# Four feature-major products of a mixer: weights or tokens stationary

## The chip, the cores and the metric

The kernel runs on one core of a Trainium2 chip. The metric is the time of one execution on the device in microseconds (us); a result is the median of several runs. All matmuls work on float32 values that are split in two parts (`wh` and `wl`, "high" and "low"), so that the tensor engine (PE) can take them in its faster float32 form: a product x·w is computed as xh·wh + xh·wl + xl·wh.

## The reference, cut to what matters

Two layers of a decoder for 256 tokens with 2048 features. Each layer has a mixer, a cross attention into 256 memory tokens, and a gated FFN. The change is in the mixer, whose input projection makes eleven things at once:

```python
z = h @ w_in
(g_q, g_k, g_v, g_r, g_lr, s_q, s_k, s_v, c_b, c_c, c_h) = split_cols(z, IN_SIZES)
o_a = gla_chunked(g_q, g_k, g_v, log_a)          # linear attention, needs g_q and g_k
o_a = rms_norm(o_a) * silu(g_r)
o_b = swa_with_sinks(rope(s_q), rope(s_k), s_v)  # softmax attention in a window
o_c = c_b * causal_dwconv(c_c * c_h, sc_conv)    # short gated convolution
return concat([o_a, o_b, o_c]) @ w_out
```

`h` is the input after an RMS norm. The kernel multiplies by the norm's row factor only after the product. g_k and g_q have 256 columns each, g_r, c_b, c_c and c_h 512 each: 2560 columns, which are the four feature-major products (keys with queries, c_c with c_h, c_b, g_r).

## The kernel before

All weights stream from memory once. `stream` loads a tile `raw` of 128 x 1024 (four buffers) on SP's DMA queue, and ACT casts it to `wh` (L160) while DVE computes `wl` (L161), three buffers each; both carry a priority.

Two forms of product use the stream. `xstat` holds 128 tokens of x as the stationary operand and lets 512 weight columns move: three matmuls for each half of the tokens and each 128 rows of K, so 6 x 16 = 96 for 512 output columns. Its result has tokens on the partitions. `wstat` holds 128 x 128 weights and lets the tokens move, high and low part of 256 tokens at once: 512 columns with `wh`, 256 with `wl`. A group of 256 output columns is 32 such pairs, and the result has features on the partitions, with the low part's share in a second half that `fold` adds (ACT copy L257, DVE add L258). `by_row` (L262) multiplies by the row factor.

Where features are wanted on the partitions after `xstat`, `turn` (L216) does it: DVE transposes blocks of 32 x 32 from PSUM (L226, two instructions for 512 columns), one DMA writes the result to DRAM (L228), and four read it back in another order (L230). `turned_by_row` (L238) multiplies by the row factor and restores the order within a row. The memory keys (`kp`), the cross queries (`qp`) and the FFN's up-projection (`up`) work so.

Small work is written as generators that `start` puts into a list of tasks. `pump` is called after each three matmuls of `xstat` and each four of `wstat`; it lets every waiting task count down by one and advances the first one that is free to its next `yield`, whose number says how many calls it then waits. `until` calls `pump` until given tasks are done. Behind all this a scheduler orders each engine's instructions at compile time; every engine then runs its own in that order.

The mixer's order is: `tokp` (columns that stay with tokens on the partitions), two `zkq` groups, two `zq` groups (softmax queries), four `zc`, two `zb`, two `zr`, then the memory keys and the output projection. `gla` (linear attention), `swa_keys`, `swa_queries`, `swa` (softmax attention) and `memory` (memory operands, loaded after the softmax tasks) run as tasks meanwhile. The uses of the feature-major groups (row factor, `conv`, gates) stand in the program right behind their product.

Of the kernel before, what the change touches and what calls it, by code (L numbers as in the profile page):

```python
# [9 lines left out]
F32 = mybir.dt.float32  # L10
# [3 lines left out]
AF = mybir.ActivationFunctionType  # L14
ALU = mybir.AluOpType
AX = mybir.AxisListType

P = 128
D = 2048
T = 256  # L20
KT = D // P
# [7 lines left out]
C_MIX, C_X, C_MEM, C_FFN = 0, 16, 32, 48  # L29
# [17 lines left out]
WPRIO = 100  # L47
# [3 lines left out]
W = dict(lr=3, gate=1, kq=7, lv=4, att=1, norm=7, kr=3, qr=4, p=8, pT=4,  # L51
         ms0=4, ms=8, xq=4, xp=8, xv=1, row=9, up=22, nx=24, up1=3, ss1=20, ss=9)
# [20 lines left out]
class Trunk:  # L73
# [24 lines left out]

    def pump(self):

        free = None
        for task in self.tasks:
            if not all(t.done for t in task.after):
                continue
            if task.wait > 0:
                task.wait -= 1
            elif free is None:
                free = task
        if free is not None:
            try:  # L110
                free.wait = (next(free.gen) or 1) - 1
            except StopIteration:
                free.done = True
                self.tasks.remove(free)

    def until(self, *tasks):
        while not all(task.done for task in tasks):
# [28 lines left out]
    def stream(self, wd, gc, kt, keep=0):  # L146
# [3 lines left out]
        for k in range(kt):  # L150
# [10 lines left out]
                    nc.vector.tensor_tensor(wl[:, :n], raw[:, :n], wh.bitcast(F32)[:, :n], ALU.subtract)  # L161
            o = (k % kp) * gc
            yield k, wh[:, o:o + gc], wl[:, o:o + gc]

    def wstat(self, xs, wd, kt=KT, name="mm", n=2):

        nc = self.nc
        ps = self.pmm.tile([P, 2, 512], F32, tag="mm", name=name)
        for k, wh, wl in self.stream(wd, n * P, kt):
            x = xs(k // 2) if callable(xs) else xs[k // 2]  # L170
            xhl = x[:, k % 2, :, :].rearrange("p a t -> p (a t)")
            xh = x[:, k % 2, 0, :]
            for m in range(n):
                ms = slice(m * P, (m + 1) * P)
                if k < kt - 1:
                    nc.tensor.matmul(ps[:, m, :], lhsT=wh[:, ms], rhs=xhl, start=(k == 0), stop=False)
                    nc.tensor.matmul(ps[:, m, 0:T], lhsT=wl[:, ms], rhs=xh, start=False, stop=False)
                else:
                    nc.tensor.matmul(ps[:, m, 0:T], lhsT=wl[:, ms], rhs=xh, start=False, stop=False)
                    nc.tensor.matmul(ps[:, m, :], lhsT=wh[:, ms], rhs=xhl, start=False, stop=True)  # L180
            self.pump()
        return ps

    def xstat(self, xs, wd, gc=512, name="mm", kt=KT):

# [60 lines left out]
            return out[j]  # L246
        return operand


    def fold(self, ps, name="z", z=None):  # L250

        nc = self.nc
        b = self.scratch(name + "_b", (P, 2, T))
        if z is None:
            z = self.ev.tile([P, 2, T], F32, tag="evz", name=name)
        with self.tc.high_priority(offset=WPRIO):
            nc.scalar.copy(b, ps[:, :, T:2 * T])  # L257
            nc.vector.tensor_tensor(z, ps[:, :, 0:T], b, ALU.add)  # L258
        return z

    def by_row(self, z, rbc):
        self.nc.vector.tensor_tensor(z, z, rbc.unsqueeze(1).broadcast_to([P, 2, T]), ALU.mult)  # L262

    def split(self, hi, lo, src):
        self.nc.scalar.copy(hi, src)
# [156 lines left out]
    def gla(self, l, tok, kq, ready, o_sb):  # L422

        nc = self.nc
# [20 lines left out]
        b = self.big("b", [P, 512])  # L445
# [1 line left out]
            s = slice(c * 64, c * 64 + 64)  # L447
            nc.vector.tensor_tensor_scan(b[:, s], mn[:, s], ab[:, s], 0.0, ALU.add, ALU.subtract)
        while not ready:
            yield 1  # L450
        yield W["kq"]
        kz, qz = kq[:, 0, :], kq[:, 1, :]
        sc = 1.0 / 16.0
# [66 lines left out]
        for hp in range(2):  # L520
            for tb in range(2):
                for par in range(2):
                    rows = slice(par * 64, par * 64 + 64)
                    nc.tensor.matmul(pb[par][0:64, hp, tb, :], lhsT=kd[rows, hp, 2 * tb, :],
                                     rhs=qd[rows, hp, 2 * tb + 1, :], start=True, stop=True)
# [9 lines left out]
        for hp in range(2):  # L535
            for par in range(2):
                rows = slice(par * 64, par * 64 + 64)
                nc.tensor.matmul(pf[par][:, hp, :], lhsT=kd[rows, hp, 0:2, :].rearrange("p c s -> p (c s)"),
                                 rhs=qd[rows, hp, 2:4, :].rearrange("p c s -> p (c s)"), start=True, stop=True)
# [17 lines left out]
        for tb in range(2):  # L557
            for hd in range(4):
                hp, par = hd // 2, hd % 2
                if tb:  # L560
                    nc.tensor.matmul(pos[1][:, hd, :], lhsT=far[:, par, hp, :], rhs=vals[0][:, hd, :],
                                     start=True, stop=False)
                nc.tensor.matmul(pos[tb][:, hd, :], lhsT=am[:, par, hp, tb, :], rhs=vals[tb][:, hd, :],
                                 start=(tb == 0), stop=True)
# [128 lines left out]
    def mixer(self, l, xs, ss, after):  # L693
        nc, a = self.nc, self.a
        tok = [self.big(f"tok{tb}", [P, 2 * TOKC]) for tb in range(2)]
        rc, rbc, rt = self.row_factor(ss, "rx", W["ss1"] if l else 1, after)
        pst = self.xstat_both(xs, a["w_tok"][l], name="tokp")
        self.layer_rest(l)
        fm = lambda g, name: self.fold(self.wstat(xs, a["w_fm"][l, g], name=name), name)
        if l:  # L700
            self.until(rt)
        with self.tc.high_priority(offset=WPRIO):
            for c in range(2):
                for tb in range(2):
                    dst = tok[tb][:, c * TOKC:(c + 1) * TOKC]
                    if l:
                        nc.scalar.activation(dst, pst[c][tb], AF.Copy, scale=rc[:, tb:tb + 1])
                    else:
                        (nc.vector.tensor_copy if tb else nc.scalar.copy)(dst, pst[c][tb])
        z0 = fm(0, "zkq")  # L710
        if l == 0:
            self.until(rt)
            for tb in range(2):
                nc.scalar.activation(tok[tb], tok[tb], AF.Copy, scale=rc[:, tb:tb + 1])
        qsc = self.par.tile([P, 4], F32, tag="qs", name="qs")
        nc.vector.tensor_scalar(qsc[:, 0:2], rc, 0.125, None, ALU.mult)
        nc.vector.tensor_scalar(qsc[:, 2:4], rc, -0.125, None, ALU.mult)
        kq, o_sb = self.big("kq", [P, 2, 512]), self.big("o", [P, 4, T])
        ready = []
        tg = self.start(self.gla(l, tok, kq, ready, o_sb))  # L720
        if l == 0:
            self.rope_tables()
        for g in range(2):
            z = fm(g, "zkq") if g else z0
            nc.vector.tensor_tensor(kq[:, g, :].rearrange("p (h t) -> p h t", h=2), z,
                                    rbc.unsqueeze(1).broadcast_to([P, 2, T]), ALU.mult)
        nc.scalar.mul(kq[:, 1, :], kq[:, 1, :], 0.125)
        ready.append(True)
        kp, vp = self.operand("kp"), self.actp.tile([P, 2, 2, 2, P], F32R, tag="act", name="vp")
        tk = self.start(self.swa_keys(tok, kp, vp))  # L730
        ob, ts = [], []
        q = [self.big("q", (P, 2, 512)) for _ in range(2)]
        self.claim(*q)
        for g in range(2):
            qs, qTs = self.swa_rope(q[g], self.xstat(xs, a["w_q"][l, g], name="zq"), qsc), []
            og = []
            ob.append(og)
            tq = self.start(self.swa_queries(qs, qTs))
            ts += [self.start(self.swa(g, n, qTs, kp, vp, og), tk, tq) for n in range(2)]
        if l == 0:  # L740
            self.tm = self.start(self.memory_factor())
        ys, oc = self.big("cy", [P, 4, T]), [self.operand(f"oc{g}") for g in range(2)]
        self.claim(ys, *oc)
        for j in range(4):
            z = fm(4 + j, "zc")
            self.by_row(z, rbc)
            self.conv(j, z[:, 0, :], z[:, 1, :], ys[:, j, :])
        ms = []
        self.start(self.memory(l, ms), *ts)
        for g in range(2):  # L750
            z = fm(8 + g, "zb")
            self.by_row(z, rbc)
            nc.vector.tensor_tensor(z, z, ys[:, 2 * g:2 * g + 2, :], ALU.mult)
            self.split(oc[g][:, :, 0, :], oc[g][:, :, 1, :], z)
        zr, oa = self.big("zr", [P, 2, 2, T]), [self.operand(f"oa{g}") for g in range(2)]
        for g in range(2):
            z = self.fold(self.wstat(xs, a["w_fm"][l, 2 + g], name="zr"), "zr", zr[:, g])
            self.by_row(z, rbc)
        ts.append(self.start(self.gla_out(o_sb, zr, oa), tg, *ts))
        return oc + oa, ob, ts, ms  # L760

    def gla_out(self, o_sb, zr, oa):

# [132 lines left out]
    def memory(self, l, ms):  # L896
        nc = self.nc
        for j in range(0, 8, 2):
            raw = self.raw.tile([P, 2, 2, T], F32, tag="raw", name="mem")
            nc.sync.dma_start(raw, self.a["mem"][j // 2])  # L900
            x = [self.operand(f"ms{j + i}") for i in range(2)]
            self.claim(*x)
            ms += x
            yield W["ms0"]
            for i in range(2):
                self.prep(raw[:, i], self.p[:, C_MEM:C_MEM + 16], j + i, x[i])
                yield W["ms"]

    def cross_keys(self, l, ms):
# [164 lines left out]
def _groups(w, gc):  # L1074

    d, k, n = w.shape
    w = w.reshape(d, k // P, P, n // gc, gc).transpose(0, 3, 2, 1, 4)
    return np.ascontiguousarray(w).reshape(d, n // gc, P, (k // P) * gc)
# [12 lines left out]
def _layout(inp):  # L1091
# [4 lines left out]
    fm = [gk, gq, gr]  # L1096
    for j in range(4):
        fm += [cc[j * P:(j + 1) * P], ch[j * P:(j + 1) * P]]
    w_in = inp["w_in"]
    d = {}  # L1100
    d["w_tok"] = _groups(w_in[:, :, np.concatenate([lr, sk, sv, gv])], 2 * TOKC)[:, 0]
    d["w_fm"] = _groups(w_in[:, :, np.concatenate(fm + [cb])], 2 * P)
    d["w_q"] = _groups(w_in[:, :, heads], 512)
    ro = np.arange(2048)
    rows = np.concatenate([ro[1536:], ro[:512],
# [60 lines left out]
```

## Time and profile before

| | |
|---|---|
| median of 3 runs | 2840.64 us (2839.71 to 2843.66) |
| profiled execution, its time | 2840.81 us |
| its span, first to last instruction | 2839.0 us |
| PE busy, DVE busy, ACT busy | 99%, 67%, 51% of the span |
| TensorE clock granted, mean | 0.998 |
| matmuls | 13554 |
| moved | 616.97 MB, mean 217 GB/s |

A matmul's drawn length overlaps that of the next, so a PE that is busy all the time may still lose time between starts. The distance between starts is what tells the rate. Waits in the profile are put down to the last semaphore that came.

### The profile page before, as it was taken

To read this page: it belongs to the slowest core of one execution; us is meant where nothing else is said; L and a number is where in the kernel's file an instruction comes from. 1 tells how busy PE (TensorE), PEld (TensorE's weight loads), DVE (VectorE), ACT (ScalarE), POOL (GpSimd) and SP (SyncE) were. 2 spreads that over 40 slices of the span, in tenths; PEclk is the share of its full clock that TensorE was granted. 3 is DMA by queue.
4 is the path that set the end of the run, shared out by engine and by line. 5 is a ranking of instruction groups with operands and counts; after the bars stand their busy time and mean duration, and the time that the engine had idled before them with its cause. 6 is when DMAs were issued, how large, how long until landed. Compare 5 with 4: busy or idle time off the path is not lost.

```text
span 2839.0 us, 37045 instructions
## 1 busy us (share of the span) xinstructions
PE 2822.7 (99%) x13554; PEld 2362.7 (83%) x13554; DVE 1888.9 (67%) x2879; ACT 1445.1 (51%) x2060; POOL 15.8 (1%) x44
## 2 busy tenths in 40 slices
PE   9999999999999999999999999999999999999998
PEld 9888888888888888888888888888888888888886
DVE  6886665556777777755568866655567777777445
ACT  6665454445555555544455644544455555555333
POOL 0000000000000000000000000000000000000001
PEclk9999999999999999999999999999999999999999
DMA  7457777657777777766664577775677777777665
GB/s 265 153 167 224 240 242 228 182 166 246 246 230 248 244 243 235 245 208 208 202 191 149 165 230 236 240 221 172 191 233 247 243 241 238 244 239 247 195 194 155
DMA packets 207030, 616.97 MB, mean 217 GB/s; under 512 B 23520, under 2 KB 65024, under 8 KB 206848
## 3 DMA queue, kind: packets, MB, share of 16 engines
q1 hardware_dynamic: 206848, 614.61, 69.0%
q8 instruction: 106, 1.74, 0.3%
q14 instruction: 76, 0.62, 0.1%
HBM read 570.48 MB, written 44.04 MB: 216 GB/s over the span
## 4 chain that ended last, share of the span: by engine, by line
PE 97%; DVE 2%; ACT 1%; DMA 0%; issue 0%; SPq 0%; ACTq 0%; DVEq 0%
PE up L194 11%; PE up L193 11%; PE up L195 11%; PE fin L832 8%; PE res L195 7%; PE res L194 7%; PE res L193 7%; PE tokp L211 2%; PE qp L194 2%; PE vp L193 2%; PE vp L195 2%; PE vp L194 2%; PE qp L193 2%; PE qp L195 2%; PE kp L195 2%; PE kp L194 2%
## 5 line engine op out<-in xcount | busy, mean ns | idle before, releaser
L161 DVE TENSOR_TENSOR wl<-raw,wh 128x1024 fp32r<-128x1024 f32 (+1 forms) x992 | 1200.1, 1212 | 781.8 <-ACT wh L160 779.9
L160 ACT CAST wh<-raw 128x1024 fp32r<-128x1024 f32 (+1 forms) x992 | 1034.8, 1045 | 1137.0 <-PE up L195 324.5
L194 PE MATMUL up<-wl,xs 128*128 128x512 f32 x1408 | 548.2, 389 | 0.0
L193 PE MATMUL up<-wh,xs 128*128 128x512 f32 x1408 | 547.8, 389 | 0.0
L195 PE MATMUL up<-wh,xs 128*128 128x512 f32 x1408 | 547.7, 389 | 0.0
L193 PEld LDWEIGHTS up<-wh,xs 128*128 128x128 f32 x1408 | 264.3, 188 | 55.2
L194 PEld LDWEIGHTS up<-wl,xs 128*128 128x128 f32 x1408 | 264.3, 188 | 55.1 <-DVE wl L161 0.5
L195 PEld LDWEIGHTS up<-wh,xs 128*128 128x128 f32 x1408 | 264.3, 188 | 54.6
L832 PE MATMUL fin<-wh,a 128*128 128x512 f32 x704 | 189.9, 389 | 0.0
L832 PEld LDWEIGHTS fin<-wh,a 128*128 128x128 f32 x704 | 132.2, 188 | 27.5
L193 PE MATMUL res<-wh,a 128*128 128x512 f32 x352 | 136.9, 389 | 0.0
L195 PE MATMUL res<-wh,a 128*128 128x512 f32 x352 | 136.9, 389 | 0.0
L194 PE MATMUL res<-wl,a 128*128 128x512 f32 x352 | 136.9, 389 | 0.0
L832 PE MATMUL fin<-wl,a 128*128 128x512 f32 x352 | 110.0, 389 | 0.0
L1028 ACT ACTIVATE u<-z_t,par 128x256 f32<-128x256 f32 x176 | 91.5, 591 | 31.5 <-DVE z_t L238 30.8
L193 PE MATMUL vp<-wh,ms 128*128 128x512 f32 x256 | 100.3, 392 | 0.0
L193 PE MATMUL qp<-wh,xs 128*128 128x512 f32 x256 | 100.2, 391 | 0.0
L194 PE MATMUL qp<-wl,xs 128*128 128x512 f32 x256 | 100.0, 390 | 0.0
L194 PE MATMUL vp<-wl,ms 128*128 128x512 f32 x256 | 99.9, 390 | 0.0
L195 PE MATMUL vp<-wh,ms 128*128 128x512 f32 x256 | 99.9, 390 | 0.0
L195 PE MATMUL qp<-wh,xs 128*128 128x512 f32 x256 | 99.8, 390 | 0.0
L193 PE MATMUL res<-wh,xo 128*128 128x512 f32 x256 | 99.6, 389 | 0.0
(318 smaller groups left out, 4309.3 us busy)
## 6 DMA issues: line engine op xcount, KB each, us to landing
raw<-in_wu SPq DMA_DIRECT2D x352, 512.0 KB, 4.6
raw<-in_wd SPq DMA_DIRECT2D x176, 512.0 KB, 4.2
raw<-in_w_fm SPq DMA_DIRECT2D x80, 512.0 KB, 4.6
raw<-in_wk SPq DMA_DIRECT2D x64, 512.0 KB, 4.0
raw<-in_wo SPq DMA_DIRECT2D x64, 512.0 KB, 4.3
raw<-in_wq SPq DMA_DIRECT2D x64, 512.0 KB, 4.3
raw<-in_wv SPq DMA_DIRECT2D x64, 512.0 KB, 3.6
raw<-in_wxo SPq DMA_DIRECT2D x64, 512.0 KB, 4.0
```

Of the source, the lines that this page charges most:

```text
L160: nc.scalar.copy(wh[:, :n], raw[:, :n])
L161: nc.vector.tensor_tensor(wl[:, :n], raw[:, :n], wh.bitcast(F32)[:, :n], ALU.subtract)
L193: nc.tensor.matmul(ps[:, tb, :gc], lhsT=xh, rhs=wh, start=(k == 0), stop=False)
L194: nc.tensor.matmul(ps[:, tb, :gc], lhsT=xh, rhs=wl, start=False, stop=False)
L195: nc.tensor.matmul(ps[:, tb, :gc], lhsT=xl, rhs=wh, start=False, stop=(k == kt - 1))
L211: nc.tensor.matmul(out[c][tb], lhsT=lhs, rhs=w[:, c * TOKC:(c + 1) * TOKC], start=(k == 0 and i == 0), stop=(k == KT - 1 and i == 2))
L832: nc.tensor.matmul(ps[c][tb], lhsT=lhs, rhs=w[v][:, c % 2 * 512:c % 2 * 512 + 512], start=(k == 0 and n == 0), stop=(k == FT - 1 and n == 2))
L1028: nc.scalar.activation(u[:, s, :], z[:, s, :], AF.Identity, bias=self.p[:, C_FB + m:C_FB + m + 1], scale=tap[2])
```

## The change

The 2560 feature-major columns are laid out in five groups of 512 instead of ten of 256, and all of them go through `xstat`, `turn` and `turned_by_row`; `wstat`, `fold` and `by_row` are gone. The uses become tasks (`gated`), which start after the row factor's task and wait `W["up"]` = 22 calls of `pump` before they touch the turned data. The order of groups becomes 0 (keys and queries), two `zq` groups, 2 and 3 (convolution), 4 (its gate), 1 (silu gate). `pump` advances up to two free tasks in a call instead of one. `gla` asks for its keys and queries every third call instead of at each. The scaling of `tok` in layer 0 becomes a task behind the row factor, and the list of memory operands is filled as each is prepared, with `mem` pumping until the one that is asked for is there. The diff, cut to its core:

```diff
     def pump(self):
-        free = None
+        free = []
         for task in self.tasks:
             if not all(t.done for t in task.after):
                 continue
             if task.wait > 0:
                 task.wait -= 1
-            elif free is None:
-                free = task
-        if free is not None:
+            elif len(free) < 2:
+                free.append(task)
+        for task in free:
...
-    def wstat(self, xs, wd, kt=KT, name="mm", n=2):
...
-    def fold(self, ps, name="z", z=None):
...
-    def by_row(self, z, rbc):
...
         while not ready:
-            yield 1
+            yield 3
...
-        z0 = fm(0, "zkq")
-        if l == 0:
-            self.until(rt)
-            for tb in range(2):
-                nc.scalar.activation(tok[tb], tok[tb], AF.Copy, scale=rc[:, tb:tb + 1])
...
+        def scales():
+            if l == 0:
+                for tb in range(2):
+                    nc.scalar.activation(tok[tb], tok[tb], AF.Copy, scale=rc[:, tb:tb + 1])
+            nc.vector.tensor_scalar(qsc[:, 0:2], rc, 0.125, None, ALU.mult)
+            nc.vector.tensor_scalar(qsc[:, 2:4], rc, -0.125, None, ALU.mult)
+            yield 1
+
+        rt = self.start(scales(), rt, first=True)
+        group = lambda g, name, then: self.start(self.gated(
+            self.turn(self.xstat(xs, a["w_fm"][l, g], name=name), name), rbc, then), rt)
...
-        for g in range(2):
-            z = fm(g, "zkq") if g else z0
-            nc.vector.tensor_tensor(kq[:, g, :].rearrange("p (h t) -> p h t", h=2), z,
-                                    rbc.unsqueeze(1).broadcast_to([P, 2, T]), ALU.mult)
-        nc.scalar.mul(kq[:, 1, :], kq[:, 1, :], 0.125)
-        ready.append(True)
+
+        def keys_queries(z):
+            yield from z(kq.rearrange("p g (h t) -> p (g h) t", h=2))
+            nc.scalar.mul(kq[:, 1, :], kq[:, 1, :], 0.125)
+            ready.append(True)
+
+        group(0, "zkq", keys_queries)
+        self.until(rt)
...
-        for j in range(4):
-            z = fm(4 + j, "zc")
-            self.by_row(z, rbc)
-            self.conv(j, z[:, 0, :], z[:, 1, :], ys[:, j, :])
+        def channels(g, z):
+            z = yield from z()
+            for i in range(2):
+                self.conv(2 * g + i, z[:, 2 * i, :], z[:, 2 * i + 1, :], ys[:, 2 * g + i, :])
+                yield 1
+
+        def gates(z):
+            z = yield from z()
+            for g in range(2):
+                w = self.scratch("zy", (P, 2, T))
+                nc.vector.tensor_tensor(w, z[:, 2 * g:2 * g + 2], ys[:, 2 * g:2 * g + 2, :], ALU.mult)
+                self.split(oc[g][:, :, 0, :], oc[g][:, :, 1, :], w)
+                yield 1
+
+        tc = [group(2 + g, "zc", lambda z, g=g: channels(g, z)) for g in range(2)]
         ms = []
         self.start(self.memory(l, ms), *ts)
-        for g in range(2):
-            z = fm(8 + g, "zb")
...
+        ts.append(group(4, "zb", gates))
...
+        tr = group(1, "zr", lambda z: z(zr.rearrange("p g h t -> p (g h) t")))
+        ts.append(self.start(self.gla_out(o_sb, zr, oa), tg, tr, *ts))
+
+        def mem(j):
+            while len(ms) <= j:
+                self.pump()
+            return ms[j]
+
+        return oc + oa, ob, ts, mem
+
+    def gated(self, turned, rbc, then):
+        zf, zt = turned
+        def fetch(z=zt):
+            yield W["up"]
+            self.turned_by_row(z, zf, rbc)
+            return z
+        yield from then(fetch)
+        yield 1
```

## Rows read from the trace of the kernel before

**Rows 1.** The page: engines' busy time, and TensorE's granted clock in 40 slices.

```profile
PE 2822.7 (99%) x13554; PEld 2362.7 (83%) x13554; DVE 1888.9 (67%) x2879; ACT 1445.1 (51%) x2060; POOL 15.8 (1%) x44
...
PEclk9999999999999999999999999999999999999999
```

**Rows 2.** Timeline of PE: start, length, line, form; four stretches' first and last.

```profile
41.95 0.39 PE L176 MATMUL zkq<-xs,wh 128*128 128x512 f32 x1
...
50.26 0.39 PE L176 MATMUL zkq<-xs,wh 128*128 128x512 f32 x1
...
739.62 0.39 PE L193 MATMUL up<-wh,xs 128*128 128x512 f32 x1
...
761.38 0.39 PE L193 MATMUL up<-wh,xs 128*128 128x512 f32 x1
...
1636.48 0.39 PE L176 MATMUL zr<-xs,wh 128*128 128x512 f32 x1
...
1644.95 0.40 PE L176 MATMUL zr<-xs,wh 128*128 128x512 f32 x1
```

**Rows 3.** Waits of PE in the whole span: us in total, times, longest.

```profile
PE zq L194 <- DVE wl L161: 1.9, 2, 1.3
...
PE zr L177 <- DVE wl L161: 0.8, 1, 0.8
PE zr L176 <- ACT wh L160: 0.4, 1, 0.4
```

**Rows 4.** Windows: us, busy PE, PEld, DVE, ACT, POOL, PEclk, DMA, GB/s.

```profile
66.00:126.00 60.00, 59.35 (x498) 48.00 (x497) 51.20 (x141) 37.81 (x82) 0.21 (x3) 1.00 0.48 148
126.00:185.00 59.00, 59.00 (x347) 51.35 (x346) 48.95 (x139) 38.71 (x89) 0.48 (x6) 1.00 0.53 170
185.00:215.00 30.00, 29.86 (x174) 25.63 (x173) 25.44 (x45) 19.14 (x36) 0.18 (x2) 1.00 0.54 169
...
700.00:1179.00 479.00, 479.00 (x2116) 396.37 (x2115) 359.40 (x535) 258.86 (x355) 0.00 (x0) 1.00 0.75 241
```

**Rows 5.** Groups by line and form, 42 to 239 us: busy us, mean ns, idle.

```profile
L161 DVE TENSOR_TENSOR wl<-raw,wh 128x1024 fp32r<-128x1024 f32 x57 | 69.3, 1220 | 19.1 <-ACT wh L160 18.9
...
L258 DVE TENSOR_TENSOR zc<-zc,zc_b 128x512 f32<-128x512 f32 x4 | 2.7, 683 | 0.1
...
L257 ACT COPY zc_b<-zc 128x512 f32<-128x512 f32 x4 | 2.3, 584 | 0.0
```

**Rows 6.** Lines 226 and 238: ns min/median/max, and DVE's idle time before.

```profile
L226 DVE STREAM_TRANSPOSE z_t<-up x88: 668/690/717, 721.5 to 2588.5; 128x512 f32<-128x512 f32 x88
...
L238 DVE TENSOR_TENSOR z_t<-z,rxb x88: 681/686/695, 732.0 to 2615.2; 128x512 f32<-128x512 f32 x88
...
  DMA z<-z_d: 38.0, 39
```

**Rows 7.** DMA issues: count, KB each, median us to landing.

```profile
z<-z_d SPq DMA_DIRECT2D x240, 128.0 KB, 3.1
```

**Rows 8.** Waits of SP's DMA queue: us in total, times, longest.

```profile
SPq L230 <- DMA z_d<-z_t: 173.0, 60, 3.8
SPq L228 <- DVE z_t L226: 79.4, 60, 2.2
```

**Rows 9.** The chain that ended last, in order of time: start, us, what.

```profile
75.22 0.50 PE a L492 x22
...
85.08 1.15 DVE wl L161
...
1482.93 1.14 DVE wl L161
```

**Rows 10.** Tile ob, the softmax attention's output: durations, first and last start.

```profile
L266 DVE TENSOR_TENSOR ob<-ov,ob x16: 411/416/425, 149.7 to 1619.4; 128x256 fp32r<-128x256 f32 x16
```

**Rows 11.** Tile ms, the memory operands: durations, first and last start.

```profile
L279 DVE SCALAR_TENSOR_TENSOR ms<-mem,par,ms x32: 472/478/485, 206.8 to 1641.0; 128x256 fp32r<-128x256 f32 x32
```

**Rows 12.** Timeline of ACT, 207 to 222 us; in brackets idle time and releaser.

```profile
217.14 1.71 ACT L278 ACTIVATE ms<-mem,par 128x256 fp32r<-128x256 f32 x4 [4.30 <-DMA mem<-in_mem]
```

More of the change, by code (lines that the diff above doesn't have):

```diff
@@ L106, in pump @@
                 task.wait -= 1
-            elif free is None:
-                free = task
-        if free is not None:
+            elif len(free) < 2:
+                free.append(task)
+        for task in free:
             try:
-                free.wait = (next(free.gen) or 1) - 1
+                task.wait = (next(task.gen) or 1) - 1
             except StopIteration:
-                free.done = True
-                self.tasks.remove(free)
+                task.done = True
+                self.tasks.remove(task)
     def until(self, *tasks):
@@ L163, in stream @@
             yield k, wh[:, o:o + gc], wl[:, o:o + gc]
-    def wstat(self, xs, wd, kt=KT, name="mm", n=2):
[L167 to L182, printed above, removed]
     def xstat(self, xs, wd, gc=512, name="mm", kt=KT):
@@ L247, in when @@
         return operand
-    def fold(self, ps, name="z", z=None):
[L252 to L259, printed above, removed]
-    def by_row(self, z, rbc):
-        self.nc.vector.tensor_tensor(z, z, rbc.unsqueeze(1).broadcast_to([P, 2, T]), ALU.mult)
     def split(self, hi, lo, src):
@@ L698, in mixer @@
         self.layer_rest(l)
-        fm = lambda g, name: self.fold(self.wstat(xs, a["w_fm"][l, g], name=name), name)
         if l:
@@ L709, in mixer @@
                         (nc.vector.tensor_copy if tb else nc.scalar.copy)(dst, pst[c][tb])
-        z0 = fm(0, "zkq")
-        if l == 0:
-            self.until(rt)
-            for tb in range(2):
-                nc.scalar.activation(tok[tb], tok[tb], AF.Copy, scale=rc[:, tb:tb + 1])
-        qsc = self.par.tile([P, 4], F32, tag="qs", name="qs")
-        nc.vector.tensor_scalar(qsc[:, 0:2], rc, 0.125, None, ALU.mult)
-        nc.vector.tensor_scalar(qsc[:, 2:4], rc, -0.125, None, ALU.mult)
+        qsc = self.par.tile([P, 4], F32, tag="qs", name="qs")
+        def scales():
[8 more added lines that the diff above has]
+            self.turn(self.xstat(xs, a["w_fm"][l, g], name=name), name), rbc, then), rt)
         kq, o_sb = self.big("kq", [P, 2, 512]), self.big("o", [P, 4, T])
         ready = []
-        tg = self.start(self.gla(l, tok, kq, ready, o_sb))
+        tg = self.start(self.gla(l, tok, kq, ready, o_sb), rt)
         if l == 0:
             self.rope_tables()
-        for g in range(2):
-            z = fm(g, "zkq") if g else z0
-            nc.vector.tensor_tensor(kq[:, g, :].rearrange("p (h t) -> p h t", h=2), z,
-                                    rbc.unsqueeze(1).broadcast_to([P, 2, T]), ALU.mult)
-        nc.scalar.mul(kq[:, 1, :], kq[:, 1, :], 0.125)
-        ready.append(True)
+        def keys_queries(z):
[4 more added lines that the diff above has]
+        self.until(rt)
         kp, vp = self.operand("kp"), self.actp.tile([P, 2, 2, 2, P], F32R, tag="act", name="vp")
-        tk = self.start(self.swa_keys(tok, kp, vp))
+        tk = self.start(self.swa_keys(tok, kp, vp), rt)
         ob, ts = [], []
@@ L743, in mixer @@
         self.claim(ys, *oc)
-        for j in range(4):
-            z = fm(4 + j, "zc")
-            self.by_row(z, rbc)
-            self.conv(j, z[:, 0, :], z[:, 1, :], ys[:, j, :])
+        def channels(g, z):
[11 more added lines that the diff above has]
+        tc = [group(2 + g, "zc", lambda z, g=g: channels(g, z)) for g in range(2)]
         ms = []
         self.start(self.memory(l, ms), *ts)
-        for g in range(2):
-            z = fm(8 + g, "zb")
-            self.by_row(z, rbc)
-            nc.vector.tensor_tensor(z, z, ys[:, 2 * g:2 * g + 2, :], ALU.mult)
-            self.split(oc[g][:, :, 0, :], oc[g][:, :, 1, :], z)
-        zr, oa = self.big("zr", [P, 2, 2, T]), [self.operand(f"oa{g}") for g in range(2)]
[L756 to L760, printed above, removed]
+        ts.append(group(4, "zb", gates))
+        zr, oa = self.big("zr", [P, 2, 2, T]), [self.operand(f"oa{g}") for g in range(2)]
+        tr = group(1, "zr", lambda z: z(zr.rearrange("p g h t -> p (g h) t")))
[13 more added lines that the diff above has]
+        yield 1
     def gla_out(self, o_sb, zr, oa):
@@ L902, in memory @@
             self.claim(*x)
-            ms += x
             yield W["ms0"]
             for i in range(2):
-                self.prep(raw[:, i], self.p[:, C_MEM:C_MEM + 16], j + i, x[i])
+                ms.append(self.prep(raw[:, i], self.p[:, C_MEM:C_MEM + 16], j + i, x[i]))
                 yield W["ms"]
@@ L1101, in _layout @@
     d["w_tok"] = _groups(w_in[:, :, np.concatenate([lr, sk, sv, gv])], 2 * TOKC)[:, 0]
-    d["w_fm"] = _groups(w_in[:, :, np.concatenate(fm + [cb])], 2 * P)
+    d["w_fm"] = _groups(w_in[:, :, np.concatenate(fm + [cb])], 512)
     d["w_q"] = _groups(w_in[:, :, heads], 512)
```

## The prediction, made before the change was run

> **What bounds the kernel now.** I read the page first: PE is busy 2822.7 of 2839.0 us [rows 1], and the granted clock is full from start to end. That row alone says only that the tensor engine sets the time; a matmul is drawn with 389 ns while the next one starts after 227 ns, so a short stall doesn't show in it. So I went to the starts of the matmuls. In the FFN's up-projection, which already has the form that the change gives to the mixer (activations stationary, 512 weight columns moving), 96 matmuls take from 739.62 to 761.38 us: 21.76 us, 226.7 ns each [rows 2]. 512 columns at the full clock of 2.4 GHz are 213.3 ns, so each matmul carries 13.4 ns beside its columns. In the mixer's feature-major groups (weights stationary) a pair of a 512-column and a 256-column matmul takes 346.3 ns in the first group (24 pairs, 41.95 to 50.26) and 352.9 ns in the last (24 pairs, 1636.48 to 1644.95) [rows 2]. Its 768 columns are 320.0 ns: two fixed parts of about 13 ns, and in some groups 6.6 ns more.
>
> The waits of PE come next. Apart from the warm-up they are 1.9 us at zq, 0.8 and 0.4 at zr: four in all, each for a split weight (the ACT cast `wh` or the DVE difference `wl`) [rows 3]. Since 389 - 227 = 162 ns of each is hidden by the drawn length, what they cost is 3.1 + 4 x 0.16 = 3.7 us. All lie in the mixer. There DVE, not the transfers, is near its limit: 51.2 of 60 us, 49.0 of 59, 25.4 of 30, against 359.4 of 479 in the FFN, where the DMA share is higher (0.75 against about 0.5) and PE waits for nothing [rows 4].
>
> So the stake is small: the matmuls' fixed parts in ten 512-column groups, and a few stalls.
>
> **The matmuls.** Removed per layer: ten 256-column groups of 32 pairs, in two layers 640 pairs (1280 matmuls). Added: five groups of 96, in two layers 960 matmuls. Both stream the same 491,520 columns, so only fixed parts differ. Bounds for a pair: 346.3 and 352.9 ns; I take the middle, 349.6, since groups of both kinds are about equally common. 640 x 0.3496 = 223.7 us go and 960 x 0.2267 = 217.6 us come: **6.1 us less** (4.0 with the lower pair, 8.2 with the upper) [rows 2].
>
> The trace prices the fixed part at 13.4 ns [rows 2]. The Trainium skill (TensorE: Matmul & The Clock Gate, section Back-to-back issue gap) speaks against the change here: it gives a warm gap of N/2.4 ns plus 2.5 ns, by which 320 instructions fewer would be worth 320 x 2.5 ns = 0.8 us, an estimate from that page. The trace doesn't agree with it: 226.7 ns at 512 columns.
>
> **The evacuation.** Removed per 256 columns: an ACT copy (584 ns), a DVE add (683) and a DVE multiply of the same shape [rows 5]. Added per 512 columns: two DVE block transposes (690 each) and two multiplies by the row factor (686) [rows 6]. DVE: 4 x 0.683 = 2.73 us before, 2 x 0.690 + 2 x 0.686 = 2.75 after: nothing. ACT: 2 x 0.584 = 1.2 us less per group, 12 us over the kernel, off the path. The keys' and queries' multiply, the convolution and the gate multiply keep their element counts. PSUM keeps two buffers of two banks; one is to be emptied in 21.8 us instead of 11.1. The two transposes need 1.4 us, so this costs nothing.
>
> **The turn through DRAM.** Ten turns more, each one write of 512 KB and four reads of 128 KB on SP's queue, behind which the weight loads stand. The reads land 3.1 us after issue [rows 7], and SP stands 173.0 us in 60 turns (2.9 each) until the write is there, 79.4 us (1.3 each) for the transposes [rows 8]. So a turn holds the weights' queue for about 4.2 us, plus the issues. Cover: four raw tiles of 2.72 us of PE each (12 matmuls), and up to three split ones. The FFN does just this every 21.8 us with no PE wait [rows 3, 4]; the mixer gets the same cadence. I take nothing; if that cover is gone, a turn costs up to its 4.2 us, 42 us in all, which the FFN's rows speak against.
>
> **The later start of the linear attention.** Its keys and queries now come whole after 41.6 + 21.8 = 63.4 us (the first pair starts 0.35 us before the 41.95 of [rows 2]), and their use waits 22 steps of three matmuls (0.68 us): 15 us, more than write and reads need, then 7 steps more: about 83 us instead of 75.2 [rows 9]. Its output is wanted by the output projection alone, which comes after the four streams of the memory keys (4 x 21.8 us), so 8 us are covered: nothing. The convolution, gate and silu groups have their results turned within the next stream; the last (zr) turns under the memory keys, 87 us long: nothing. The tok scaling of layer 0 moves behind the row factor; its bound is the one wait at zq that it adjoins, 1.3 us.
>
> **Two tasks at each step.** The step hands out work; it adds none. Attention chains that shared one slot now advance together, so the softmax ends earlier (in layer 1 its last output came at 1619.4 us [rows 10]), and the memory operands, which wait for it and were prepared until 1641.0 us [rows 11], 4 us before the last zr matmuls of [rows 2] end, come earlier: a wait less likely, never seen here. The price is order: DVE and ACT run theirs in a fixed order. At 217 us ACT stood 4.3 us for a load of `mem` [rows 12], the casts of `wh` behind it came late, and PE paid the zr waits. Such stalls are bounded below by none (3.7 us gained) and above by the rivals. As DVE's load stays the same and ACT's falls slightly, I take about as much stall as before: 0.
>
> Sum: -6.1 us. The profiled execution took 2840.81 us, 0.17 above the median: 2840.81 - 6.1 = 2834.7, as a median 2834.5 us (-0.22%). Less than 0.2%, 5.7 us, is about what can't be told from no change.
>
> **Rivals.**
> *Stalls vanish.* Earlier use and less ACT work keep `wh` and `wl` ahead: -6.1 - 3.7 = -9.8, 2831. For it: the FFN runs this form clean [rows 3]. Against: the mixer's DVE share, 83 to 85% against 75% [rows 4].
> *The wait for turned data takes the gain.* The multiply by the row factor waits for the reads on DVE: 39 times, 38.0 us, in the kernel before [rows 6]; `wl` queues behind it. If half of the ten turns lose what the late `mem` did (0.8 + 0.4 + 0.3 = 1.5 us), it is 7.5 us: 2842, no change.
> *DVE is overrun: slower.* Splitting weights takes DVE 69.3 us of the 197 from 42 to 239 [rows 5], 21 us in each 60, so tasks are 30 of the 51.2 us in 66 to 126 and 28 of the 49.0 in 126 to 185 [rows 4]. Two tasks at a time pull the second share forward. A third of it (9 us) just fills the first stretch; with half, 5 us spill over, in both layers 10; with two thirds, 10 and 20: 2840.6 - 6.1 + 20 = 2854. It decides from half on. For it: at 85 us and 1482 us, where PE waited for zq, the chain that ended last runs through DVE's `wl` [rows 9]. Against: the splits have priority, so the work that spills is the tasks' own.
> *The new form runs slower in the mixer.* If its matmuls there take 233 ns, as the pairs of the last group are slower than those of the first by 6.6 [rows 2], 960 of them need 223.7 us and nothing is won: 2840.6, no change. Against: none of the FFN's do. The Trainium skill's 2.5 ns of the page above would end at the same place (2839.8 us, by its 0.8 us).
>
> **Chances.** Stalls as before, within 2 us: 0.41, of which 0.24 lie beyond -5.7 us. Stalls gone: 0.24. Turned data late: 0.20. DVE overrun: 0.12. Slower matmuls: 0.03. Faster 0.24 + 0.24 = 0.48; no change 0.17 + 0.20 + 0.03 = 0.40; slower 0.12. The range: down to 2828.5 (no stalls with the upper pair: 2840.6 - 8.2 - 3.7), up to 2846, which holds the late data and the overrun up to half; the rest of the overrun is left out. The likeliest case alone: 2830.5 to 2838.5.
>
> **What would show it.** 20 transposes and 20 more multiplies by the row factor, 70 writes and 280 reads of turned data; no fold; 96 matmuls in 21.8 us in each quiet group; the first product of the linear attention near 83 us; the softmax's last output of layer 1 well before 1619 us. Wrong would be: pairs' fixed part not the cause (groups slower than 21.8 us without a wait), PE waits for `wl` or `wh` above 10 us, or PE waiting for `ms` at the start of the memory keys.

## The result and the profile after

The changed kernel takes 2855.24 us (median of 6 runs, 2854.09 to 2856.39), the kernel before, beside it, 2839.69 (2839.40 to 2843.66): a ratio of 1.0054, 95% interval 1.0044 to 1.0064. It is slower by half a per cent. The prediction (2834.5, range 2828.5 to 2846) had the wrong sign, and the measured time lies outside the range.

The profiled spans are 2839.0 us before and 2853.0 after. The first part of the page, after:

```profile
PE 2829.8 (99%) x13234; PEld 2353.6 (82%) x13234; DVE 1890.7 (66%) x2879; ACT 1435.6 (50%) x2040; POOL 15.8 (1%) x44
```

320 matmuls are gone as planned, DVE's work is the same and ACT's is 10 us less [rows 1]. The span is 14 us longer with less to do, so the loss is in waits and in the rate. The waits of PE, after, apart from the warm-up (us in total, times, longest):

```profile
PE zr L175 <- DVE wl L161: 4.0, 2, 2.6
PE zr L174 <- ACT wh L160: 2.4, 2, 1.6
PE zc L175 <- DVE wl L161: 2.3, 1, 2.3
PE zq L175 <- DVE wl L161: 0.9, 1, 0.9
PE zb L175 <- DVE wl L161: 0.6, 1, 0.6
PE zc L174 <- ACT wh L160: 0.5, 1, 0.5
```

Against [rows 3]: zr had 1.2 us and has 6.4; zc and zb had none. Around the waits at zc (142.9 us) and at zr (231.6 us; 1643 and 1646 us) the granted clock falls. Windows after (us, PE, PEld, DVE, ACT and POOL busy, clock, DMA share, GB/s):

```profile
118.00:139.00 21.00, 20.46 (x150) 15.73 (x148) 14.64 (x46) 14.30 (x45) 0.35 (x3) 1.00 0.47 151
139.00:146.00 7.00, 4.44 (x12) 2.95 (x11) 7.00 (x17) 4.54 (x8) 0.00 (x0) 0.55 0.54 153
232.00:235.00 3.00, 3.00 (x9) 2.32 (x8) 3.00 (x5) 2.41 (x4) 0.00 (x0) 0.50 0.97 272
1645.00:1651.00 6.00, 4.82 (x11) 3.80 (x12) 6.00 (x9) 3.12 (x5) 0.00 (x0) 0.50 0.68 216
```

At 0.50 (1.2 GHz) a matmul of 512 columns starts 0.43 us after the last, where 0.23 us is usual at the full clock. The timeline of PE after shows it behind the wait at zc, and, in a quiet stretch of the keys' group, two rows that are 12 matmuls apart: 2.72 us, 226.7 ns each:

```profile
59.13 0.39 PE L176 MATMUL zkq<-wh,xs 128*128 128x512 f32 x1
...
61.85 0.39 PE L176 MATMUL zkq<-wh,xs 128*128 128x512 f32 x1
...
142.86 0.80 PE L175 MATMUL zc<-wl,xs 128*128 128x512 f32 x1 [2.26 <-DVE wl L161]
143.45 0.63 PE L176 MATMUL zc<-wh,xs 128*128 128x512 f32 x1
143.88 0.63 PE L174 MATMUL zc<-wh,xs 128*128 128x512 f32 x1
```

I set the distance from each matmul's start to the next against (columns + 32)/2.4 GHz, which gives 226.7 ns at 512 columns, and added up the excess. The span's +14.0 us divide so:

| | before | after | difference, us |
|---|---|---|---|
| fixed parts: 320 matmuls fewer at 13.3 ns | | | -4.3 |
| excess where PE waited | 4.6 | 13.0 | +8.3 |
| excess in the three stretches at half clock (17 us long) | 0 | 6.1 | +6.1 |
| excess between small matmuls of tasks | 8.9 | 13.9 | +5.0 |
| excess within the ten feature-major groups | 4.5 | 4.7 | +0.2 |
| all else | | | -1.3 |

The fourth line holds no wait that the profile shows. It grows where two tasks' matmuls alternate. In layer 1, after, one transpose of the softmax (`pT`, 128 columns) and then two to four products of the linear attention (`a`, 32 columns) follow each other at 0.20 to 0.26 us, where (columns + 32)/2.4 GHz gives 0.07 us for a transpose and 0.03 for a product; 22 such products in one run took 0.50 us before [rows 9]. That the switch itself costs is an argument: a wait shorter than the drawn length doesn't show here.

```profile
1554.38 0.27 PE L645 MATMUL pT<-con,pr 128*128 128x128 f32 x1
1554.58 0.30 PE L459 MATMUL a<-e 64*64 64x32 f32 x4
1554.82 0.33 PE L645 MATMUL pT<-con,pr 128*128 128x128 f32 x1
1555.08 0.30 PE L459 MATMUL a<-e 64*64 64x32 f32 x2
1555.31 0.33 PE L645 MATMUL pT<-con,pr 128*128 128x128 f32 x1
```

**What comes later.** The tile `ob`, after (durations, first to last start):

```profile
L233 DVE TENSOR_TENSOR ob<-ov,ob x16: 414/418/425, 159.8 to 1649.9; 128x256 fp32r<-128x256 f32 x16
```

And the splits of the memory operands `ms`, in the view of the tile `mem`:

```profile
L246 DVE SCALAR_TENSOR_TENSOR ms<-mem,par,ms x32: 473/478/485, 224.2 to 1654.7; 128x256 fp32r<-128x256 f32 x32
```

The softmax's last output came at 1619.4 [rows 10] and comes at 1649.9; the memory operands' last split came at 1641.0 [rows 11] and comes at 1654.7. In layer 0 the linear attention's products `a` end at 165.3 us instead of 108.9, the last `ob` is at 236.5 instead of 213.8, the first `ms` at 223.5 instead of 205.2, while the memory keys start only 11 us later (246.7 for 235.7).

**The wait at zc (142 us).** ACT's groups after, 129.5 to 137.5 us: sixteen exponentials, each with a read of its sum, in a row:

```profile
L631 ACT ACTIVATE pr<-pr,swc 128x256 f32<-128x256 f32 x8 | 4.0, 501 | 0.0
L631 ACT ACTIVATE pr<-pr,swc 128x128 f32<-128x128 f32 x8 | 3.1, 388 | 0.0
L631 ACT ACTIVATION_READ_ACCUMULATOR pr<-pr,swc 128x1 f32 x16 | 3.0, 190 | 0.0
```

The cast before them began at 129.13, the next at 137.56, though its raw tile had landed at 132.96. Three split buffers are 3 x 2.72 = 8.2 us of PE; the distance is 8.4 us here and up to 10.7 elsewhere, before never above 8.2.

The longer part of the wait is DVE's. PE took the cast at 138.65 us, ran four transposes and then stood 2.26 us for `wl`, until 142.86. DVE ran eight scalings of the softmax (`pr`) and four operations of the linear attention (`e`) first:

```profile
138.13 2.19 DVE L638 TENSOR_SCALAR pr<-pr,swc 128x256 f32<-128x256 f32 x8
140.24 0.42 DVE L440 TENSOR_TENSOR e<-b 128x256 f32<-128x256 f32 x1
...
141.58 1.22 DVE L161 TENSOR_TENSOR wl<-raw,wh 128x1024 fp32r<-128x1024 f32 x1
```

So it is at all five waits for `wl`, 7.8 us of the 10.7: the cast was done 0.7 to 3.0 us before DVE began on `wl`, and DVE did tasks' work or stood for turned data in between.

**The waits at zr.** The timeline of ACT, after, around 220 us:

```profile
217.85 1.05 ACT L160 CAST wh<-raw 128x1024 fp32r<-128x1024 f32 x1 [1.12 <-PE zb L176]
223.02 0.58 ACT L232 CAST pT<-pT 128x512 fp32r<-128x512 f32 x1 [4.12 <-PE pT L645]
223.50 2.91 ACT L245 ACTIVATE ms<-mem,par 128x256 fp32r<-128x256 f32 x7
...
226.57 2.11 ACT L245 ACTIVATE ms<-mem,par 128x256 fp32r<-128x256 f32 x5
228.58 2.12 ACT L160 CAST wh<-raw 128x1024 fp32r<-128x1024 f32 x2
```

And SP's, of the same stretch:

```profile
216.77 0.33 SPq L897 DMA_DIRECT2D mem<-in_mem  x1
219.52 0.33 SPq L209 DMA_DIRECT2D zb_d<-zb_t  x1
220.62 0.48 SPq L158 DMA_DIRECT2D raw<-in_w_fm  x1
222.69 1.75 SPq L211 DMA_DIRECT2D zb<-zb_d  x4
225.94 5.96 SPq L158 DMA_DIRECT2D raw<-in_w_fm  x4
```

Three loads of `mem` (issued at 170.9, 196.6 and 216.8 us) sit in three of the four raw buffers until their twelve preparations run, in a row, from 223.50 to 228.7. One buffer is left for weights: one load goes out at 220.62, the next at 225.94, after the turn of zb. No weight is cast between 217.85 and 228.58. Before, at most two were lent, and the preparations came as 8, 4 and 4.

In layer 1, at 1646.18 us, `wl` came late for turned data as well. ACT had ended the cast at 1643.06; DVE then stood for the reads of zb and multiplied them by the row factor before it split:

```profile
1637.96 4.83 DVE L246 SCALAR_TENSOR_TENSOR ms<-mem,par,ms 128x256 fp32r<-128x256 f32 x12
1643.70 1.29 DVE L219 TENSOR_TENSOR zb_t<-zb,rxb 128x512 f32<-128x512 f32 x2 [0.90 <-DMA zb<-zb_d]
1644.91 1.22 DVE L161 TENSOR_TENSOR wl<-raw,wh 128x1024 fp32r<-128x1024 f32 x1
```

### The profile page after: what moved, and what is told of

Its sections match the earlier page's. It is cut to its first block, busy times and chain, and to the rows that moved or that the text cites. A ratio compares the mean times of both kernels' runs of the same rounds, so it can differ in the third digit from the quotient of the medians.

```text
span 2853.0 us, 36449 instructions
## 1 busy us (share of the span) xinstructions
PE 2829.8 (99%) x13234; PEld 2353.6 (82%) x13234; DVE 1890.7 (66%) x2879; ACT 1435.6 (50%) x2040; POOL 15.8 (1%) x44
## 4 chain that ended last, share of the span: by engine, by line
PE 96%; DVE 1%; ACT 1%; DMA 1%; issue 0%; SPq 0%; ACTq 0%; DVEq 0%
PE up L175 11%; PE up L176 11%; PE up L174 11%; PE fin L829 8%; PE res L176 7%; PE res L174 7%; PE res L175 7%; PE tokp L192 2%; PE qp L175 2%; PE vp L175 2%; PE vp L174 2%; PE qp L176 2%; PE vp L176 2%; PE qp L174 2%; PE kp L174 2%; PE kp L175 2%
## 5 line engine op out<-in xcount | busy, mean ns | idle before, releaser
L174 PE MATMUL vp<-wh,ms 128*128 128x512 f32 x256 | 100.2, 392 | 0.0
L174 PE MATMUL qp<-wh,xs 128*128 128x512 f32 x256 | 100.2, 391 | 0.0
```

Source lines behind the costliest of these rows:

```text
L174: nc.tensor.matmul(ps[:, tb, :gc], lhsT=xh, rhs=wh, start=(k == 0), stop=False)
```

## The experiments

The theories. **Order:** two tasks a step and the later use of the keys let small work come in rows that outlast the split buffers (theory P of the expectations). **Lent buffers:** `mem` and `memt` hold raw buffers that the weights need (theory R). **Queue:** ten more turns stand between weight loads on SP (theory T). **Form:** the product is itself slower here. Each kernel has 3 rounds, and its ratio is to the kernel before beside it (2839.4 to 2840.5 us).

**One part alone.** `one_task`: the new form, one task a step; its linear attention still asks for its keys every third call. `two_before`: the old form, two tasks, and asking every third call.

```diff
# one_task, on the kernel after
-elif len(free) < 2:
+elif len(free) < 1:
# two_before, on the kernel before
-elif free is None:
-    free = task
+elif len(free) < 2:
+    free.append(task)
...
-    yield 1
+    yield 3
```

> The changed kernel with one task advanced at a step instead of two; products and turns stay. Its PE waits are 10.7 us and three stretches at half clock cost about 8.5 us more. Theory R (weight tiles starve because memory loads sit in the stream's raw buffers while ACT is late): fewer late preparations, PE waits of 3 to 7 us, 2838 to 2848. Rival P (two tasks at a step bunch the work on ACT and DVE): the stalls go back to those of the kernel before, 2833 to 2840. Rival T (the turns hold the weights' queue): stalls stay, above 2850.

> The kernel before, weights stationary, with two tasks advanced at a step and the linear attention asking every third call. Theory P: the stalls come with the two tasks, 2848 to 2860. Theory T: the stalls need the turns, so no change, 2836 to 2843. Theory R alone: some more waits because the memory loads come earlier, 2840 to 2850.

Measured: 2846.27 (1.0021 [1.0012, 1.0030]) and 2848.59 (1.0031 [1.0019, 1.0043]). Each part alone costs, 6.6 and 8.9 us, and their sum is the 15.5 us of the change. That is no proof that they are independent: asking every third call is in both kernels, the excess between small matmuls rises by 0.4 us in `two_before` and 2.0 in `one_task`, but by 5.0 with both, and with five raw buffers (below) the two don't add up. In `two_before` PE waits 4.2 us at zc in two waits; the longer (2.9) comes behind two casts at 1526.33 and 1538.28 with sixteen exponentials between them. So the two tasks cost without the new form, and the late `mem` is not needed for it.

**The raw buffers.** `raw5` has five of them, `mem_own` four and one more for `mem` and `memt` alone; `before_raw5` (with two `evz` buffers, to make room) and `before_raw3` do it to the kernel before, `one_raw5` to `one_task`.

```diff
-self.raw = pool("raw", 4)
+self.raw = pool("raw", 5)
-... self.raw.tile([P, 2, 2, T], F32, tag="raw", name="mem")
+... self.raw.tile([P, 2, 2, T], F32, tag="mem", name="mem", bufs=1)
```

> The changed kernel with five raw buffers instead of four, the memory loads still among them. Theory R: one more weight tile ahead while memory tiles are held, the waits fall by about half, 2840 to 2850. Rival P: 2850 to 2857, since ACT is late whatever is loaded. Rival T: a turn of 4.2 us on the queue is then covered, 2836 to 2845.

> The changed kernel with one buffer of its own for the memory loads (mem and memt), so that the four raw buffers hold weights alone. Theory R: the waits of PE for wh and wl at zc and zr fall from 9.8 us to under 4, the clock stays at full, 2835 to 2843. Rivals P and T: ACT and DVE are as bunched, the queue as held, 2850 to 2857.

> The kernel before with five raw buffers (and two instead of three for the sums of fold, to make room). If a fifth raw tile helps any form of this kernel, its own 3.1 us of waits for split weights go and it takes 2835 to 2838; if the shortage came only with the change, 2838.5 to 2841.

> The changed kernel with one task at a step and five raw buffers. Two tasks at a step cost 9 us with either form, the fifth buffer gave 14 us with two tasks. Theory R (starved weights are the common path of both): the waits fall below 4 us, nothing at half clock, and the 4.3 us of fewer fixed parts show: 2834 to 2839. Rival P (work bunched on ACT and DVE, which one task already undoes): no more from the buffer, 2843 to 2847.

> The kernel before with three raw buffers instead of four. Theory R: a memory load then leaves two for the weights, as the changed kernel with two held, so PE waits for wh and wl where mem and memt are under way (140 to 235 us and 1583 to 1640 us): 2846 to 2860. If raw buffers matter only with the turns: under 2844.

| | one task | two tasks |
|---|---|---|
| old form, four raw | 2839.7 | 2848.6 |
| old form, five raw | 2840.0 | 2854.5 |
| new form, four raw | 2846.3 | 2855.2 |
| new form, five raw | 2837.6 | 2841.5 |

`raw5`: 1.0005 [0.9996, 1.0015]; `mem_own` 2845.42, 1.0020 [1.0010, 1.0029]; `before_raw5` 1.0000 [0.9990, 1.0009]; `one_raw5` 0.9991 [0.9982, 1.0001]. The fifth buffer takes 13.8 us off the change and nothing off the kernel before. `raw5` has no stretch at half clock ahead of its last 9 us; the excess of its waits is 5.5 us instead of 13.0, and that between small matmuls stays (14.4). Its main waits of PE:

```profile
PE zr L175 <- DVE wl L161: 2.4, 2, 1.2
PE kp L175 <- DVE wl L161: 1.2, 1, 1.2
```

In `raw5` the longest distances between two casts are 9.6, 9.0 and 8.9 us, about those of the changed kernel (10.7, 9.5, 9.0), so such rows on ACT alone don't make the loss. With a buffer of its own `mem` gives back 9.8 us, and waits for split weights come at kp: each load of `mem` must wait for the last to be used up, and in layer 0 the last memory operand is prepared at 245.5 us, after the keys' stream has begun (239.9). In `one_raw5`, the new form with one task, the time is 2.0 us under the kernel before beside it, which the interval doesn't tell from none. The excess of the small matmuls is 9.3 us, and what PE still waits for is mostly at zq:

```profile
PE zq L175 <- DVE wl L161: 3.1, 3, 2.0
```

`before_raw3` takes 2912.09 (1.0252 [1.0237, 1.0267]), far more than was expected and in another place: most of its waits lie in the FFN, fifty of at most 0.9 us:

```profile
PE up L194 <- DVE wl L161: 29.9, 50, 0.9
```

So one raw buffer less costs the kernel 72 us, most of it in a group that turns its result: the four of the prediction's cover are needed, not spare. A sixth buffer:

> The changed kernel with six raw buffers. With five it took 2841.5 us with 5.6 us of waits left. Theory R: the weights have what they need even with three memory tiles held, waits under 3 us: 2836 to 2840. If what is left is the order on ACT and DVE: 2840 to 2843, as with five.

> The changed kernel with one task at a step and six raw buffers. With five it took 2837.6 us, 6.9 us of it waits (4 of them for split weights in the mixer). Theory R: fewer of them, 2833 to 2837. If what is left is the order on DVE and ACT: 2837 to 2840.

2840.98 (1.0006 [0.9996, 1.0015]) and 2837.97 (0.9994 [0.9984, 1.0003]): nothing more.

**Own buffer and fifth one.** `own_raw5` and `one_own_raw5` have five raw buffers for weights and one for `mem`.

> The changed kernel, two tasks at a step, with five raw buffers for weights alone and one for the memory loads. Theory R: waits as with six shared, under 4 us, 2837 to 2842. As with the own buffer at one task a step (2847.6), the memory operands may come late for the keys' stream: then PE waits at kp, 2842 to 2848.

> The changed kernel with one task at a step, five raw buffers for weights alone and one for the memory loads: as much memory as six shared ones. Theory R: as six shared ones or better, 2833 to 2837. If a single buffer delays the memory operands until the keys' stream wants them: PE waits at kp, 2838 to 2846.

2842.22 (1.0010 [1.0000, 1.0019]) and 2847.59 (1.0025 [1.0016, 1.0034]): no better than `raw5` (0.8 us more) and worse than `one_raw5` by 10.0 us. In `one_own_raw5` kp waits 2.2 us for `wl` and 1.0 for `wh`. That the memory loads want several buffers early as much as the weights do is read from these waits, which are less than the 10 us.

**The queue.** `turn_pool` moves the added turns' writes and reads to GpSimd's queue.

```diff
+q = nc.gpsimd if name in ("zkq", "zc", "zb", "zr") else nc.sync
-nc.sync.dma_start(zd...
+q.dma_start(zd...
```

> The changed kernel with the ten added turns issued on POOL's queue, so that no weight load stands behind one. Theory T (the turns hold the weights' queue): the waits at zr in both layers, 6.4 us with 5 us of half clock, go: 2841 to 2848. Theory R (the raw buffers that memory loads hold): they stay held, 2850 to 2857.

2860.17 (1.0073 [1.0058, 1.0088]). The waits at zr are still there, and one for the keys is new:

```profile
PE zr L175 <- DVE wl L161: 3.7, 4, 2.0
PE zr L174 <- ACT wh L160: 3.7, 2, 1.9
PE a L460 <- ACT kq L698: 3.1, 1, 3.1
```

The queue theory, as the cause by itself, falls.

**The order.** `two_before_raw5` tests whether the fifth buffer heals the two tasks in the old form; `solo_raw5` advances no second task in a step that linear attention takes; `seq_two_before`, `seq_after` and `seq_raw5` put a layer's four softmax tasks one behind the other.

```diff
-ts += [self.start(self.swa(g, n, qTs, kp, vp, og), tk, tq) for n in range(2)]
+for n in range(2):
+    ts.append(self.start(self.swa(g, n, qTs, kp, vp, og), tk, tq, *ts[-1:]))
```

> The kernel before with two tasks at a step, the linear attention asking every third call, and five raw buffers (two instead of three for the sums of fold). Theory R: the 9 us that two tasks cost are starved weights as well, 2838 to 2843. Theory P: they are the order of the work on ACT and DVE, whatever is loaded, 2846 to 2851.

> The kernel before with two tasks at a step, the four softmax tasks of a layer one after the other. Theory P (two softmax tasks side by side make ACT run sixteen exponentials between two weight casts): the longest distance between two casts falls from 11.9 us to about 8, the 3.1 us wait at zc goes, 2838 to 2842. Theory R or another: as with the softmax tasks side by side, 2846 to 2851.

> The changed kernel with the four softmax tasks of a layer one after the other. Theory P: the wait at zc (2.8 us and a stretch at half clock of 6.8 us) goes; those at zr, where twelve preparations of memory operands stand in a row, stay or come later: 2845 to 2851. Theory R alone: 2852 to 2858.

> The same with five raw buffers. Both together: neither long rows of exponentials nor held weight tiles, waits under 5 us, 2835 to 2839, no worse than one task at a step (2837.6). If running the softmax in turn makes the memory operands late: PE waits at kp, 2840 to 2846.

> The changed kernel with five raw buffers and two tasks at a step, but the linear attention's steps alone. Two tasks at a step with five took 2841.5 us, one 2837.6. If what the second slot still costs is the mixing of the linear attention's small matmuls with the softmax's: 2836 to 2839. If it is the softmax's and memory's own bunching: 2840 to 2843.

`two_before_raw5`: 2854.50 (1.0051 [1.0034, 1.0068]); it is not healed, and zc in layer 1 waits 4.2 us as without the buffer. In layer 0 a transpose of the softmax waits 1.9 us for the scaled `pr`; ACT from 172 to 182 us shows the sixteen exponentials again:

```profile
L664 ACT ACTIVATE pr<-pr,swc 128x256 f32<-128x256 f32 x8 | 4.0, 497 | 2.8 <-DVE swc L659 2.8
L664 ACT ACTIVATE pr<-pr,swc 128x128 f32<-128x128 f32 x8 | 3.1, 387 | 0.0
```

`seq_two_before`: 2848.55 (1.0029 [1.0016, 1.0042]). The wait at zc is all but gone (0.3 us), as the theory of order asked, but the longest distance between two casts fell from 11.9 to 10.3 us only, not to 8, and 2.7 us at `ov` and 1.9 at zr come for it: no gain. `seq_after`: 2869.66 (1.0106 [1.0091, 1.0121]), with zc healed too and the end of the mixer worse, since the softmax, and with it `mem`, is later still:

```profile
PE zr L175 <- DVE wl L161: 5.6, 2, 3.4
PE zr L174 <- ACT wh L160: 3.8, 3, 1.9
PE kp L174 <- ACT wh L160: 3.1, 1, 3.1
```

With five buffers it is 2851.74 (`seq_raw5`, 1.0043 [1.0028, 1.0058]), `solo_raw5` 2847.37 (1.0025 [1.0015, 1.0035]), both worse than `raw5` and outside what was expected of them.

**The late keys.** `early_keys` gives the keys' group 14 calls of wait instead of 22 and linear attention 2 instead of 7.

```diff
-rbc, then), rt)
+rbc, then, 14 if g == 0 else W["up"]), rt)
-kq=7, lv=4
+kq=2, lv=4
```

> The changed kernel with the keys' and queries' group waiting 14 calls instead of 22 for its turned data and the linear attention 2 instead of 7 behind it, so that its first product comes at about 76 us instead of 82. Theory L (the 8 us of delay push the linear attention into the softmax, both then take far longer, and the memory operands come too late for the last group): the last product before 130 us, memory operands by 212 us, waits at zr gone or halved, 2842 to 2849. Rival P (the overlap comes from two tasks at a step): the chain shifts by a few us only, 2851 to 2857.

2855.42 (1.0049 [1.0033, 1.0066]): no gain. The products `a` of the linear attention end at 125 us instead of 165, and the excess between small matmuls falls by 4 to 5 us, about back to that of the kernel before: this bears out that it comes with the overlap of linear attention and softmax. The waits at zr are halved (3.2 us for 6.4), as expected. But waits in other places take their place, since 14 calls are too few for the turn in layer 1: DVE stands 6.0 us there for the turned keys, until 1492.4 us, and the next `wl` (1496.7) comes behind the linear attention's work:

```profile
PE zq L175 <- DVE wl L161: 3.7, 2, 2.9
PE a L459 <- ACT kq L697: 2.9, 2, 2.0
```

## Why the prediction was wrong

*The matmuls* (-6.1): right in sign, too large. 226.7 ns holds in quiet stretches (the rows at 59.13 and 61.85), but over all ten groups, waits and half clock aside, a pair before took 353.7 ns and a matmul after 231.6 on average: 640 x 0.3537 - 960 x 0.2316 = 226.4 - 222.3 = 4.1 us less, about the lower bound of the step. The 7 ns by which most pairs were above two fixed parts were no property of the pair: 5 ns of the kind stay with each new matmul. The fixed part is 13.3 ns all the same. By the N/2.4 ns plus 2.5 ns that the Trainium skill (TensorE: Matmul & The Clock Gate, section Back-to-back issue gap) gives for isolated warm matmuls the quiet rows would be 215.8 ns apart, an estimate from that page; they are 226.7 ns apart.

*Evacuation* (0) and *DVE's load* held, to 2 us of DVE and -10 of ACT.

*The turn through DRAM* (0): the cover named was "four raw tiles". This step failed, mainly in its cover: the memory loads take up to three of the four. The FFN, which I took as proof of the cadence, lends none, and with three buffers it waits 29.9 us. The fifth buffer (-13.8 us in the new form, 0 in the old) shows that the new form needs the cover that it lost; moving the turns off the queue alone doesn't return it. The 1.3 us that bounded the moved scaling of layer 0 belong to a wait of layer 1 (at 1484 us); in layer 0 it was 0.7 us before and is 0.9 after.

*The later start of the linear attention* (0, "8 us are covered"): the start was right (82 us for 83), the cover was wrong. I asked who reads its output and not what runs when it ends. Before, the softmax's scores began at 109.0 us, as the products `a` ended (108.9); after, they begin at 105.4 and `a` goes on to 165. Both now share DVE, ACT and PE: the last `ob` comes 23 us later, the first `ms` 18 us later, and the preparations fall in a row into the last zr group, just where the lent buffers are missed.

*Two tasks at each step* (0, softmax earlier): failed. It costs 8.9 us by itself on the old form, where rows of small work on ACT and DVE stand before the casts and splits in the order that the compiler fixed, in spite of their priority. That these rows are the cause there is read from the trace; the one run that parted them (`seq_two_before`) gained nothing. The softmax ended later, not earlier.

The rival *DVE is overrun* gave 2854 and a chance of 0.12. Its number was near by luck, as it was the sum for two thirds of a second task's work spilling over, and DVE's busy time from 66 to 185 us fell, from 100.2 to 89.2 us. Its mechanism is there in part: 7.8 of the 10.7 us of waits are for `wl`, with DVE on tasks' work or turned data while the cast lay ready. What spoke against it, that the splits have priority, failed. *Turned data waits* is there in small: at 1646 us `wl` came behind a multiply that had stood 0.9 us for its reads, and in `one_task` 1.8 us at the same place, ahead of its longest wait (2.8 us); PE itself waits for turned data at the keys alone, in two variants. *Slower form* doesn't explain the loss: the groups' own excess rose by 0.2 us. The sign of being wrong that I had named, PE waits for `wl` or `wh` above 10 us, came (10.7 by the rows). Half clock around such waits was in no step and cost 6.1 us. The lower end of the range, 2840.6 - 8.2 - 3.7, is 2828.7 and not 2828.5, which changes nothing.

Open: why the fifth buffer saves most of the two tasks' cost in the new form (3.9 us left) and none in the old (14.5). No single wait carries it; each variant is ordered anew at compile time, and the waits move with it. `two_before_raw5` has one buffer more than `two_before` and takes 5.9 us longer, so a difference of some 6 us between two variants may be the order alone. The fifth buffer's gain in the new form, 13.8 us with two tasks and 8.7 with one, is above that. That the delay and the lent buffers make the zr waits is read from the rows and borne out by `raw5` and `mem_own`, but `early_keys` moved other waits in and so doesn't show the delay's share.

## What to carry to other kernels

A stall-free stretch elsewhere proves a cadence only for its own buffers: list who else takes tiles from the pool, and for how long, in the stretch that changes. When a task is delayed, ask what it will then run beside, not only who reads its result; and for in-order engines look at what stands between two casts and between a cast and its split, whatever their priority. Where PE is 99% busy, a gain of a few us in fixed parts can be lost to three waits, as here.

## What the runs showed of the hardware

Around PE waits of 1.4 to 2.6 us in a stream that is otherwise full, the granted clock stood at 0.50 (1.2 GHz) for 3.4 to 6.8 us: 17 us in all, 6.1 us lost beside the waits themselves. The kernel before, whose longest wait in the stream is 1.3 us, shows no such stretch ahead of its last 10 us, and neither does `raw5` (longest 1.2). It is no rule of a wait's length alone: `one_task` waited 2.2 us at 170 and 2.8 us at 1638 at the full clock, and had 3.4 us of half clock at a wait of 2.0; `raw6` had 3.4 us of it at 136 us beside waits of 0.6 and 0.8. Where a transpose and a run of two to four products of 32 columns alternated, each step took 0.20 to 0.26 us, while 22 such products in one run took 0.50 us [rows 9].
